# Gate and up projections as seven products of quarters

## The chip, the cores and the metric

The kernel runs on one core of a Trainium2 chip. The metric is the device time of one execution in microseconds (us). TensorE multiplies matrices into PSUM, VectorE, ScalarE and GpSimd (POOL in the profile) work on SBUF, the first two on PSUM as well, and SyncE (SP) issues the transfers from HBM. All five run on their own and wait for each other by semaphores.

## The reference

Two post-norm layers on 512 tokens of 1024 channels. Each layer has one projection with sparse attention and spatial gating, an output projection, a layer norm, then a feed-forward part of width 2816 with a gated term beside it, and a second layer norm:

```
x = layer_norm(ALPHA * x + mix, ln1_g, ln1_b)
gate, up = split(x @ w_ffn_in, 2)            # w_ffn_in: 1024 x 5632
ffn = (silu(gate) * up) @ w_ffn_out          # w_ffn_out: 2816 x 1024
ple = (p @ w_ple) * sigmoid(x @ w_ple_gate)
x = layer_norm(ALPHA * x + ffn + ple, ln2_g, ln2_b)
```

## The kernel before

All matmuls keep nearly float32 accuracy by splitting each operand into a high part (a rounded copy, type float32r) and a low part (the rest), and adding three products: high x high, high x low, low x high. `mm3` issues the three. The weights are split on the chip: `split` takes up to 1024 columns of a loaded tile, ScalarE casts the high part (`wh`), and VectorE or GpSimd subtracts it from the source to get the low part (`wl`). Activations are held transposed, channels on partitions and tokens along the columns, with both parts (`Rows`).

`ffn_in(j)` (11 times in a layer) computes 256 channels of the hidden layer: two loads of 1 MB (256 columns of gate and of up), four splits of 8 x 128 columns, for each of two channel tiles one bank of PSUM for gate and one for up, each the sum of 8 x 3 matmuls of 512 tokens. ScalarE takes Silu of gate, VectorE multiplies with up, and the product is split into the tiles `HT`. `ffn_out(f0, f1, last)` multiplies a group of hidden tiles with their rows of w_ffn_out, two halves of 512 output columns, each over four token blocks, and VectorE adds the banks into `X`. The groups are 8, 8 and 6 tiles, after passes 4, 8 and 10 of `ffn_in`. Ahead of the first pass stands the gate projection (`evac_g`, two halves of 512 columns), and ahead of that `evac_o1`, which normalizes a token block and transposes it into `X1T`.

Tiles come from pools: 15 big tiles (128 x 2048), 10 pages (128 x 512), two raw tiles for loaded weights, four pairs of `wh` and `wl`, four PSUM banks `acc` and three `ps`. Nothing is issued while the program is written down: `Order` records every operation, and `issue` then chooses the order of each engine by a list schedule. An operation has a key, the sum of the estimated TensorE time recorded before it; each engine takes, of those that could start within a short window of the earliest, the one with the lowest key. Tiles of one pool are given out in the order of the keys of their first operations. The order so found is fixed, and each engine runs through its own list, waiting where an operand is not there. All instructions are issued from one line of `issue`, so the profile shows L272 nearly everywhere, and rows are told apart by their tiles.

Of the kernel before, what the change touches and what calls it, by code (L numbers as in the profile page):

```python
# [326 lines left out]
def body(ctx: ExitStack, tc: tile.TileContext, x, p, positions, w_in, w_o, ln1_g, ln1_b,  # L327
# [20 lines left out]
    def ACC():  # L348
        return psum.tile([128, 512], F32, name="acc", tag="acc", bufs=4)
# [10 lines left out]
    def low(eng, dst, src, hi):  # L360
        eng.tensor_tensor(out=dst, in0=src, in1=f32(hi), op=OP.subtract)
# [113 lines left out]
    def wrows(w, r0, nkt, c0, c1):  # L475
        return w[r0:r0 + nkt * 128, c0:c1].rearrange("(k p) n -> p k n", p=128)

    def mform(xt, kts, load, ncols, order, evac, eng, c0=None, subs=None):


        ready = subs is not None
        subs = subs or []

        def fetch(i):
            if ready:
                return
            ks = kts[4 * i:4 * i + 4]
            rv = load(ks)
            for j in range(0, len(ks), 2):
                kk = ks[j:j + 2]  # L490
                subs.append((kk, split(rv[:, j:j + len(kk), :], [len(kk), ncols], eng)))

        nf = (len(kts) + 3) // 4

        def piece(b, acc, si):
            kk, (h, l) = subs[si]
            o = c0(b) if c0 else 0
            for j, k in enumerate(kk):
                mm3(acc[:, o:ncols], xt(k, b), (h[:, j, o:], l[:, j, o:]),
                    k == kts[0], k == kts[-1])  # L500

        if order == "k":
            accs = None
            done = 0
            for i in range(nf):
                fetch(i)
                if accs is None:
                    accs = [ACC() for _ in range(NB)]
                while done < len(subs):
                    for b in range(NB):  # L510
                        piece(b, accs[b], done)
                        if subs[done][0][-1] == kts[-1]:
                            evac(b, accs[b])
                        yield
                    done += 1
        else:
            for i in range(nf):
                fetch(i)
            for b in range(NB):
                acc = ACC()  # L520
                for si in range(len(subs)):
                    piece(b, acc, si)
                    if si == len(subs) - 1:
                        evac(b, acc)
                    yield

    def drive(main, *sides):
# [40 lines left out]
    def transpose_rows(R, b, src, halves=(0, 1)):  # L568
        for half in halves:
            ps = PS()  # L570
            for j in range(4):
                k = half * 4 + j
                PE.transpose(ps[:, j * 128:(j + 1) * 128], src[:, k * 128:(k + 1) * 128], ident)
            v = ps.rearrange("p (k t) -> p k t", k=4)
            s = slice(b * 128, (b + 1) * 128)
            A.copy(R.h[half][:, :, s], v)
            low(V, R.l[half][:, :, s], v, R.h[half][:, :, s])

    def rstd_of(src, n):

# [76 lines left out]
    for ly in range(DEPTH):  # L657
# [328 lines left out]
        X1T = Rows("x1t")  # L986

        def evac_o1(b, acc):
            xb = Xb(b)
            V.tensor_tensor(out=xb[:, 512:], in0=acc, in1=xb[:, 512:], op=OP.add)  # L990
            finish(layer_norm(xb, DM, lnp[:, 0], lnp[:, 1]))
            transpose_rows(X1T, b, xb)

        finish(mform(MT, [0, 1, 2, 3], load_o(1), 512, "b", evac_o1, G))

# [1 line left out]
        for n in range(2):  # L997
            cs = slice(n * 512, (n + 1) * 512)

            def evac_g(b, acc, n=n, cs=cs):  # L1000
                sg = PG(F32, "sg")
                A.activation(sg, acc, AF.Sigmoid)
                V.tensor_tensor(out=sg, in0=sg, in1=PLE[n][:, b], op=OP.mult)
                V.scalar_tensor_tensor(Xb(b)[:, cs], Xb(b)[:, cs], ALPHA, sg, op0=OP.mult, op1=OP.add)

            finish(mform(X1T, K8, mload(wg_l, n * 512, n * 512 + 512), 512,
                         "b" if n == 0 else "k", evac_g, G if n == 0 else V))


        HT = {}  # L1010

        def ffn_in(j):
            gr = raw(lambda t: [(t.rearrange("p (k n) -> p k n", k=8),
                                 wrows(wf_l, 0, 8, j * 256, j * 256 + 256))])
            ur = raw(lambda t: [(t.rearrange("p (k n) -> p k n", k=8),
                                 wrows(wf_l, 0, 8, DFF + j * 256, DFF + j * 256 + 256))])
            for e in range(2):
                f = 2 * j + e
                if f % 4 == 0:
                    HT[f // 4] = [T(FR, "HT").rearrange("p (k t) -> p k t", k=4) for _ in range(2)]  # L1020
                hh, hl = HT[f // 4]
                accs = []
                for r in (gr, ur):
                    w = split(r.rearrange("p (k n) -> p k n", k=8)[:, :, e * 128:e * 128 + 128],
                              [8, 128], V)
                    acc = ACC()
                    for k in range(8):
                        mm3(acc, (w[0][:, k], w[1][:, k]), X1T.all(k), k == 0, k == 7)
                    if not accs:
                        sg = PG(F32, "sg")  # L1030
                        A.activation(sg, acc, AF.Silu)
                    accs.append(acc)
                V.tensor_tensor(out=sg, in0=accs[1], in1=sg, op=OP.mult)
                A.copy(hh[:, f % 4], sg)
                low(V, hl[:, f % 4], sg, hh[:, f % 4])

        def hrow(f, b):
            bs = slice(b * 128, (b + 1) * 128)
            return HT[f // 4][0][:, f % 4, bs], HT[f // 4][1][:, f % 4, bs]

        def ffn_out(f0, f1, last):
            for n in range(2):
                cs = slice(n * 512, (n + 1) * 512)

                def evac_f(b, acc, n=n, cs=cs):
                    xb = Xb(b)
                    V.tensor_tensor(out=xb[:, cs], in0=acc, in1=xb[:, cs], op=OP.add)
                    if last and n == 1:
                        end = ly == DEPTH - 1
                        for c in layer_norm(xb, DM, lnp2[:, 0], lnp2[:, 1], 2 if end else 1):  # L1050
                            if end:
                                SY.dma_start(out[0, b * 128:(b + 1) * 128, c], xb[:, c])
                        if not end:
                            transpose_rows(XT, b, xb)

                finish(mform(hrow, list(range(f0, f1)), mload(wfo_l, n * 512, n * 512 + 512), 512,
                             "b" if last and n else "k", evac_f, G if last else V))

        for j in range(5):
            ffn_in(j)  # L1060
        ffn_out(0, 8, False)
        for j in range(5, 9):
            ffn_in(j)
        ffn_out(8, 16, False)
        for j in range(9, 11):
            ffn_in(j)
        lnp2 = T(F32, "lnp").rearrange("p (e c) -> p e c", e=2)
        row_bcast(lnp2[:, 0], ln2_g[ly], DM)
        row_bcast(lnp2[:, 1], ln2_b[ly], DM)
        if ly < DEPTH - 1:  # L1070
            subs_a = list(split_a([load_a(ly + 1, i) for i in range(2)], [V] * 4))
            XT = Rows("xt")
        ffn_out(16, 22, True)

    with tc.manual_schedule():
        order.issue()
# [22 lines left out]
```

## Time and profile before

| | |
|---|---|
| median of 3 runs | 1244.28 us (1243.76 to 1251.37) |
| profiled execution | 1247.03 us |
| its span, first to last instruction | 1245.3 us |
| mean granted clock of TensorE | 0.995 |
| TensorE, VectorE, ScalarE, GpSimd busy | 98%, 55%, 38%, 19% |
| read from HBM | 114.86 MB |

The span is that of the one profiled execution; its device time is 1.7 us longer. Busy shares are means over stages that differ, and a TensorE that is busy need not be at its full pace, since matmuls overlap in the records: one of 512 columns is shown with 389 ns while the next starts much sooner.

### The profile page before, as it was taken

Reading aid. Unit: us, or ns where it says so; the run is one execution under the profiler, and the core shown is the slowest. Engines: PE = TensorE matmul, PEld = TensorE weight load, DVE = VectorE, ACT = ScalarE, POOL = GpSimd, SP = SyncE. Lnnn points to the kernel's source line nnn. Section 1 sums busy time; section 2 is a strip of 40 time slices with the busy share of each in tenths; the row PEclk is TensorE's granted clock in tenths of the full one; section 3 lists DMA queues with packets and bytes.
Section 4 is the critical chain, followed back from the end, with each engine's and each line's share of the span. In section 5 each row is a group of like instructions: output and inputs, shape, how many; then the busy total and the mean of one; then the engine's idle time right before and its main releaser. Section 6 shows DMA issues by size and latency. Waiting matters only on the chain. (4 is left out here: it accounts for less than half of the span.)

```text
span 1245.3 us, 14733 instructions
## 1 busy us (share of the span) xinstructions
PE 1218.6 (98%) x5742; PEld 1008.8 (81%) x5742; DVE 683.7 (55%) x1334; ACT 473.5 (38%) x818; POOL 237.0 (19%) x186
## 2 busy tenths in 40 slices
PE   8989989999999999999999999999999999999997
PEld 8778768888888888888788888788888888888885
DVE  5699987853333333233487999785433333333317
ACT  5554686332222222213335558923322222222220
POOL 4135434400000000000552453460000000000042
PEclk9999999999999999999999999999999999999999
DMA  7123231242322323323411223313332324223231
GB/s 212 43 93 102 69 85 68 68 136 69 119 86 100 102 71 132 102 89 107 166 54 50 87 85 69 102 68 102 103 101 84 120 68 135 68 104 99 89 115 68
DMA packets 89621, 117.90 MB, mean 95 GB/s; under 512 B 5072, under 2 KB 59344, under 8 KB 89552
## 3 DMA queue, kind: packets, MB, share of 16 engines
q1 hardware_dynamic: 89552, 116.97, 29.5%
q8 instruction: 45, 0.74, 0.2%
q14 instruction: 24, 0.20, 0.1%
HBM read 114.86 MB, written 2.10 MB: 94 GB/s over the span
## 5 line engine op out<-in xcount | busy, mean ns | idle before, releaser
L272 POOL TENSOR_TENSOR wl<-raw,wh 128x512 fp32r<-128x512 f32 x132 | 181.6, 1403 | 888.9 <-ACT wh L272 877.0
L272 ACT CAST wh<-raw 128x1024 fp32r<-128x1024 f32 x194 | 202.8, 1050 | 382.3 <-PE acc L272 336.5
L272 DVE TENSOR_TENSOR wl<-raw,wh 128x1024 fp32r<-128x1024 f32 x128 | 156.8, 1225 | 307.5 <-ACT wh L272 307.3
L272 PE MATMUL acc<-x1th,wh 128*128 128x512 f32 x704 | 273.9, 389 | 0.0
L272 PE MATMUL acc<-x1tl,wh 128*128 128x512 f32 x704 | 273.9, 389 | 0.0
L272 PE MATMUL acc<-x1th,wl 128*128 128x512 f32 x704 | 273.9, 389 | 0.0
L272 PE MATMUL acc<-wh,HT 128*128 128x512 f32 x704 | 217.9, 389 | 0.5 <-ACT wh L272 0.5
L272 PEld LDWEIGHTS acc<-wh,HT 128*128 128x128 f32 x704 | 132.0, 188 | 28.1 <-ACT wh L272 0.9
L272 PEld LDWEIGHTS acc<-x1tl,wh 128*128 128x128 f32 x704 | 132.1, 188 | 27.6
L272 PEld LDWEIGHTS acc<-x1th,wl 128*128 128x128 f32 x704 | 132.1, 188 | 27.4
L272 PEld LDWEIGHTS acc<-x1th,wh 128*128 128x128 f32 x704 | 132.1, 188 | 27.3
L272 PE MATMUL acc<-wl,HT 128*128 128x512 f32 x352 | 137.3, 390 | 0.2 <-POOL wl L272 0.2
L272 ACT ACTIVATE sg<-acc 128x512 f32<-128x512 f32 x60 | 35.9, 598 | 189.7 <-PE acc L272 189.7
L272 DVE TENSOR_TENSOR sg<-acc,sg 128x512 f32<-128x512 f32 x44 | 30.4, 692 | 134.0 <-PE acc L272 134.0
L272 PE MATMUL acc<-wh,xth 128*128 128x512 f32 x192 | 76.3, 402 | 3.4 <-ACT rq L272 2.1
L272 PEld LDWEIGHTS acc<-wl,HT 128*128 128x128 f32 x352 | 66.1, 188 | 14.6 <-POOL wl L272 0.9
L272 PE MATMUL acc<-wl,xth 128*128 128x512 f32 x192 | 76.0, 398 | 0.0
L272 PE MATMUL acc<-wh,xtl 128*128 128x512 f32 x192 | 75.9, 396 | 0.0
L272 DVE TENSOR_TENSOR X<-acc,X 128x512 f32<-128x512 f32 x64 | 43.2, 685 | 43.5 <-PE acc L272 43.3
L272 DVE MATCH_REPLACE8 sc<-m,sc 128x384 f32<-128x384 f32 (+2 forms) x96 | 51.6, 541 | 0.0
L272 PE MATMUL acc<-wh,mth 128*128 128x512 f32 x128 | 51.3, 401 | 0.0
L272 PE MATMUL acc<-wh,mtl 128*128 128x512 f32 x128 | 51.3, 401 | 0.0
(197 smaller groups left out, 1705.4 us busy)
## 6 DMA issues: line engine op xcount, KB each, us to landing
raw<-in_w_ffn_in SPq DMA_DIRECT2D x44, 1024.0 KB, 5.1
raw<-in_w_ffn_out SPq DMA_DIRECT2D x20, 1024.0 KB, 5.0
raw<-in_w_in SPq DMA_DIRECT2D x12, 1024.0 KB, 5.3
raw<-in_w_ple_gate SPq DMA_DIRECT2D x8, 1024.0 KB, 5.0
raw<-in_w_o SPq DMA_DIRECT2D x4, 1024.0 KB, 5.3
raw<-in_w_o SPq DMA_DIRECT2D x8, 512.0 KB, 7.3
raw<-in_w_in SPq DMA_DIRECT2D x8, 324.0 KB, 4.7
X<-in_x SPq DMA_DIRECT2D x8, 256.0 KB, 5.1
```

Source lines behind the costliest of these rows:

```text
L272: o.ins = o.fn(*o.a, **o.k)
```

## The change

The input of the feed-forward part, X, is cut into four quarters: x11, x12 are the two channel halves of tokens 0 to 255, x21, x22 those of tokens 256 to 511. The weights of one pass are cut likewise: w11 and w21 are the channel halves of its 256 gate columns, w12 and w22 those of its 256 up columns. Instead of the eight products of quarters, seven are formed, from sums of quarters (the Winograd form of Strassen's scheme). The sums of X are made once in a layer (`combine`, beside the gate projection); those of the weights in every pass on VectorE, two into a new big tile `tt` and two in place over the raw tiles. A product is 2 channel tiles x 4 channel blocks x 3 matmuls of 256 tokens, its two channel tiles side by side in one bank. Bank `ba` takes four products in a row without being cleared; what it holds in between is copied or added out. `X1T` becomes an object `Quarters`, whose transposes also keep unsplit copies (`x1r`) until the sums are made. HT has one big tile for each pass. The down projection is done in groups of 6, 6, 4 and 6 tiles after passes 3, 6, 8 and 10 (counted from 0), all but the last with low parts on VectorE; the last group's loads and splits (`prefetch`, low parts on GpSimd) are recorded ahead of the next layer's first weights.

```diff
+    class Quarters:
+        def __init__(self):
+            self.q = [[self.tile("x1q") for _ in range(2)] for _ in range(2)]
+            self.raw = [T(F32, "x1r").rearrange("p (i k t) -> p i k t", i=4, k=4) for _ in range(2)]
...
+        def parts(self, t, i, src):
+            s = slice(i * 128, i * 128 + 128)
+            A.copy(t[:, 0, :, s], src)
+            low(V, t[:, 1, :, s], src, t[:, 0, :, s])
+        def rows(self, b, src):
...
+                self.parts(self.q[b // 2][half], i, v)
+                if b // 2 and half:
+                    V.tensor_tensor(out=self.raw[i][:, 3], in0=v, in1=self.raw[i][:, 2], op=OP.subtract)
+                else:
+                    A.copy(self.raw[i][:, 2 if b // 2 else half], v)
+        def combine(self):
+            self.sums = [self.tile("x1s") for _ in range(4)]
+            for i in range(2):
+                q11, q12, q21, p1 = (self.raw[i][:, j] for j in range(4))
+                self.parts(self.sums[0], i, p1)
+                yield
...
+                V.scalar_tensor_tensor(s2, p1, -1.0, q11, op0=OP.mult, op1=OP.subtract)
+                self.parts(self.sums[1], i, s2)
+                yield
+                V.tensor_tensor(out=s3, in0=q11, in1=q21, op=OP.subtract)
+                self.parts(self.sums[2], i, s3)
+                yield
+                V.scalar_tensor_tensor(s4, s2, -1.0, q12, op0=OP.mult, op1=OP.subtract)
+                self.parts(self.sums[3], i, s4)
+                yield
...
-            transpose_rows(X1T, b, xb)
+            X1T.rows(b, xb)
...
+            drive(mform(X1T, K8, mload(wg_l, n * 512, n * 512 + 512), 512,
+                        "b" if n == 0 else "k", evac_g, G if n == 0 else V), (comb, 0.25, 4))
+        finish(comb)
...
         def ffn_in(j):
...
+            w11, w21, w12, w22 = gr[:, 0:1024], gr[:, 1024:], ur[:, 0:1024], ur[:, 1024:]
+            tt = T(F32, "tt")
+            t1, t2 = tt[:, 0:1024], tt[:, 1024:]
+            t3, t4 = w12, w21
+            x11, x12, x22 = X1T.q[0][0], X1T.q[0][1], X1T.q[1][1]
+            xp, xs2, xs3, xs4 = X1T.sums
...
+            def product(bank, src, x, first):
+                h, l = split(src.rearrange("p (k n) -> p k n", k=4), [4, 256], V)
+                for e in range(2):
+                    dst = bank[:, e * 256:(e + 1) * 256]
+                    for k in range(4):
+                        cs = slice(e * 128, (e + 1) * 128)
+                        for n, (w_, x_) in enumerate(((h, 0), (h, 1), (l, 0))):
+                            PE.matmul(dst, w_[:, k, cs], x[:, x_, k], start=first and e + k + n == 0,
+                                      stop=k == 3 and n == 2, skip_group_check=True)
...
+            product(ba, w11, x11, True)
+            s1 = page_()
+            A.copy(s1, ba)
+            product(bb, w21, x12, True)
+            g1 = page_()
+            V.tensor_tensor(out=g1, in0=bb, in1=s1, op=OP.add)
+            A.activation(g1, g1, AF.Silu)
+            add(t1, w11, w12)
+            add(t2, t1, w22)
+            product(ba, t2, xs2, False)
+            s2 = page_()
+            A.copy(s2, ba)
+            bc = ACC()
+            product(bc, t1, xp, True)
+            s5 = page_()
+            A.copy(s5, bc)
+            add(t3, w22, w12)
+            product(ba, t3, xs3, False)
+            V.tensor_tensor(out=s5, in0=ba, in1=s5, op=OP.add)
+            product(bc, w22, xs4, False)
+            V.tensor_tensor(out=s2, in0=bc, in1=s2, op=OP.add)
+            add(t4, t2, w21)
+            product(ba, t4, x22, False)
+            g2 = page_()
+            A.activation(g2, ba, AF.Silu)
+            ht = HT[j] = T(FR, "HT").rearrange("p (e f t) -> p e f t", e=2, f=2)
+            for i, (g, u) in enumerate(((g1, s2), (g2, s5))):
+                V.scalar_tensor_tensor(u, u, -1.0, g, op0=OP.mult, op1=OP.mult)
+                v, ts = u.rearrange("p (f t) -> p f t", f=2), slice(i * 256, (i + 1) * 256)
+                A.copy(ht[:, 0, :, ts], v)
+                low(V, ht[:, 1, :, ts], v, ht[:, 0, :, ts])
...
+        for j in range(4):
             ffn_in(j)
-        ffn_out(0, 8, False)
-        for j in range(5, 9):
+        ffn_out(0, 6, False)
+        for j in range(4, 7):
             ffn_in(j)
-        ffn_out(8, 16, False)
+        ffn_out(6, 12, False)
+        for j in range(7, 9):
+            ffn_in(j)
+        ffn_out(12, 16, False)
         for j in range(9, 11):
             ffn_in(j)
...
+        subs_o = [prefetch(load_fo(n), list(range(16, 22)), 512, G) for n in range(2)]
...
-        ffn_out(16, 22, True)
+        ffn_out(16, 22, True, subs_o)
```

## Rows read from the trace of the kernel before

**Rows 1.** The page, busy us, share of the span and instructions of each engine.
```profile
PE 1218.6 (98%) x5742; PEld 1008.8 (81%) x5742; DVE 683.7 (55%) x1334; ACT 473.5 (38%) x818; POOL 237.0 (19%) x186
```

**Rows 2.** Windows: busy time by engine, over gate and up, then a down projection.
```profile
core 0: us, PE busy (x) PEld busy (x) DVE busy (x) ACT busy (x) POOL busy (x), PEclk, DMA share, GB/s
271.00:380.00 109.00, 109.00 (x483) 90.25 (x482) 39.17 (x43) 32.56 (x42) 0.00 (x0) 1.00 0.32 105
380.00:431.00 51.00, 51.00 (x227) 42.23 (x226) 17.48 (x19) 11.25 (x12) 0.00 (x0) 1.00 0.31 103
```

**Rows 3.** Timeline (start, duration, engine) of TensorE: first and last of 92 matmuls.
```profile
469.22 0.39 PE L272 MATMUL acc<-x1tl,wh 128*128 128x512 f32 x1
...
489.85 0.39 PE L272 MATMUL acc<-x1th,wl 128*128 128x512 f32 x1
```

**Rows 4.** Timeline of TensorE, two runs of matmuls of 256 columns.
```profile
119.17 2.67 PE L272 MATMUL ps<-vn,wsT 128*128 128x256 f32 x21
...
810.02 2.07 PE L272 MATMUL po<-PT,VV 128*128 128x256 f32 x16
```

**Rows 5.** Timeline of the weight loads: those of the second run, and one.
```profile
809.56 0.19 PEld L272 LDWEIGHTS acc<-wh,mtl 128*128 128x128 f32 x1
809.79 2.09 PEld L272 LDWEIGHTS po<-PT,VV 128*128 128x128 f32 x16
```

**Rows 6.** Timeline of VectorE around `ffn_in`, and two operations on one block.
```profile
442.20 1.23 DVE L272 TENSOR_TENSOR wl<-raw,wh 128x1024 fp32r<-128x1024 f32 x1 [4.32 <-ACT wh L272]
...
446.99 1.22 DVE L272 TENSOR_TENSOR wl<-raw,wh 128x1024 fp32r<-128x1024 f32 x1 [0.22 <-ACT wh L272]
448.13 0.68 DVE L272 TENSOR_TENSOR HT<-sg,HT 128x512 fp32r<-128x512 f32 x1
...
222.94 1.27 DVE L272 TENSOR_TENSOR x1tl<-ps,x1th 128x512 fp32r<-128x512 f32 x2
```

**Rows 7.** Timeline of ScalarE in the same stretch.
```profile
445.90 1.05 ACT L272 CAST wh<-raw 128x1024 fp32r<-128x1024 f32 x1 [3.73 <-PE acc L272]
446.86 0.62 ACT L272 CAST HT<-sg 128x512 fp32r<-128x512 f32 x1
```

**Rows 8.** Timeline of SP's queue, a load issued in the same stretch.
```profile
443.46 0.37 SPq L272 DMA_DIRECT2D raw<-in_w_ffn_in  x1
```

**Rows 9.** The page, DMA issues: count, KB each, median us from issue to landing.
```profile
raw<-in_w_ffn_in SPq DMA_DIRECT2D x44, 1024.0 KB, 5.1
```

**Rows 10.** Groups of instructions with busy us and mean ns: transposes into X1T.
```profile
L272 ACT CAST x1th<-ps 128x512 fp32r<-128x512 f32 x16 | 8.6, 590 | 28.8 <-PE ps L272 28.7
...
L272 DVE TENSOR_TENSOR x1tl<-ps,x1th 128x512 fp32r<-128x512 f32 x16 | 10.2, 680 | 0.0
```

**Rows 11.** Windows over the gate projection of the first layer.
```profile
230.00:241.60 11.60, 11.35 (x58) 9.23 (x57) 11.50 (x17) 4.87 (x8) 5.80 (x4) 1.00 0.26 90
241.60:245.40 3.80, 3.80 (x18) 3.14 (x18) 0.04 (x1) 0.60 (x1) 0.00 (x0) 1.00 0.00 0
245.40:271.00 25.60, 25.60 (x115) 21.19 (x114) 13.14 (x15) 9.43 (x11) 0.00 (x0) 1.00 0.30 91
```

**Rows 12.** Timeline of TensorE in that stretch, its one wait.
```profile
231.08 0.49 PE L272 MATMUL acc<-wh,x1tl 128*128 128x512 f32 x1 [0.25 <-DVE x1tl L272]
```

**Rows 13.** Timeline of SP's queue before the first layer's last down projection.
```profile
574.01 6.70 SPq L272 DMA_DIRECT2D raw<-in_w_in  x8
...
592.61 0.38 SPq L272 DMA_DIRECT2D raw<-in_w_ffn_out  x1
```

**Rows 14.** Timeline of ScalarE there, the casts of that load.
```profile
597.73 2.94 ACT L272 CAST wh<-raw 128x1024 fp32r<-128x1024 f32 x3 [3.99 <-DMA raw<-in_w_ffn_out]
```

**Rows 15.** Timeline of TensorE there, its longest wait.
```profile
598.83 1.20 PE L272 MATMUL acc<-wh,HT 128*128 128x512 f32 x4 [0.47 <-ACT wh L272]
```

**Rows 16.** Timeline of TensorE after its longest wait in the first projections.
```profile
71.77 0.79 PE L272 MATMUL acc<-wh,xth 128*128 128x512 f32 x1 [2.08 <-ACT rq L272]
```

**Rows 17.** Windows over that stretch; the 0.50 is the granted clock.
```profile
71.70:74.90 3.20, 3.13 (x7) 2.48 (x8) 3.20 (x12) 0.02 (x1) 1.51 (x2) 0.50 0.22 19
```

More of the change, by code (lines that the diff above doesn't have):

```diff
@@ L525, in mform, with prefetch @@
                     yield
+    def prefetch(load, kts, ncols, eng):
+        subs = []
+        for i in range(0, len(kts), 4):
+            ks = kts[i:i + 4]
+            rv = load(ks)
+            for j in range(0, len(ks), 2):
+                kk = ks[j:j + 2]
+                subs.append((kk, split(rv[:, j:j + len(kk), :], [len(kk), ncols], eng)))
+        return subs
     def drive(main, *sides):
@@ L577, in transpose_rows, with tile, __call__ @@
             low(V, R.l[half][:, :, s], v, R.h[half][:, :, s])
+    class Quarters:
+        def __init__(self):
+            self.q = [[self.tile("x1q") for _ in range(2)] for _ in range(2)]
+            self.raw = [T(F32, "x1r").rearrange("p (i k t) -> p i k t", i=4, k=4) for _ in range(2)]
+            self.sums = None
+        def tile(self, name):
+            return T(FR, name).rearrange("p (e k t) -> p e k t", e=2, k=4)
+        def __call__(self, k, b):
+            t, s = self.q[b // 2][k // 4], slice(b % 2 * 128, b % 2 * 128 + 128)
+            return t[:, 0, k % 4, s], t[:, 1, k % 4, s]
+        def parts(self, t, i, src):
[3 more added lines that the diff above has]
+        def rows(self, b, src):
+            i = b % 2
+            for half in range(2):
+                ps = PS()
+                for j in range(4):
+                    k = half * 4 + j
+                    PE.transpose(ps[:, j * 128:(j + 1) * 128], src[:, k * 128:(k + 1) * 128], ident)
+                v = ps.rearrange("p (k t) -> p k t", k=4)
+                self.parts(self.q[b // 2][half], i, v)
[9 more added lines that the diff above has]
+                yield
+                s2, s3, s4 = (PG(F32, "s").rearrange("p (k t) -> p k t", k=4) for _ in range(3))
+                V.scalar_tensor_tensor(s2, p1, -1.0, q11, op0=OP.mult, op1=OP.subtract)
[7 more added lines that the diff above has]
+                yield
     def rstd_of(src, n):
@@ L985, in body @@
         finish(mform(MT, [0, 1, 2, 3], load_o(0), 512, "b", evac_o0, G))
-        X1T = Rows("x1t")
+        X1T = Quarters()
         def evac_o1(b, acc):
@@ L1004, in evac_g @@
                 V.scalar_tensor_tensor(Xb(b)[:, cs], Xb(b)[:, cs], ALPHA, sg, op0=OP.mult, op1=OP.add)
-            finish(mform(X1T, K8, mload(wg_l, n * 512, n * 512 + 512), 512,
-                         "b" if n == 0 else "k", evac_g, G if n == 0 else V))
+            if n == 0:
+                comb = X1T.combine()
+            drive(mform(X1T, K8, mload(wg_l, n * 512, n * 512 + 512), 512,
+                        "b" if n == 0 else "k", evac_g, G if n == 0 else V), (comb, 0.25, 4))
+        finish(comb)
@@ L1010, in body @@
         HT = {}
         def ffn_in(j):
-            gr = raw(lambda t: [(t.rearrange("p (k n) -> p k n", k=8),
-                                 wrows(wf_l, 0, 8, j * 256, j * 256 + 256))])
+            c0 = j * 256
+            gr = raw(lambda t: [(t.rearrange("p (k n) -> p k n", k=8), wrows(wf_l, 0, 8, c0, c0 + 256))])
             ur = raw(lambda t: [(t.rearrange("p (k n) -> p k n", k=8),
[L1016 to L1035, printed above, removed]
@@ new lines, in ffn_in, with add @@
+                                 wrows(wf_l, 0, 8, DFF + c0, DFF + c0 + 256))])
+            w11, w21, w12, w22 = gr[:, 0:1024], gr[:, 1024:], ur[:, 0:1024], ur[:, 1024:]
[4 more added lines that the diff above has]
+            xp, xs2, xs3, xs4 = X1T.sums
+            def add(out, a, b):
+                V.tensor_tensor(out=out, in0=a, in1=b, op=OP.add)
+            def product(bank, src, x, first):
[7 more added lines that the diff above has]
+                                      stop=k == 3 and n == 2, skip_group_check=True)
@@ new lines, in page_ @@
+            def page_():
+                return PG(F32, "fg")
+            ba, bb, bc = ACC(), ACC(), None
+            product(ba, w11, x11, True)
[9 more added lines that the diff above has]
+            s2 = page_()
@@ L1037, in hrow @@
+            ht = HT[j] = T(FR, "HT").rearrange("p (e f t) -> p e f t", e=2, f=2)
[4 more added lines that the diff above has]
+                low(V, ht[:, 1, :, ts], v, ht[:, 0, :, ts])
         def hrow(f, b):
             bs = slice(b * 128, (b + 1) * 128)
-            return HT[f // 4][0][:, f % 4, bs], HT[f // 4][1][:, f % 4, bs]
@@ L1041, in ffn_out, with load_fo @@
-        def ffn_out(f0, f1, last):
+            return HT[f // 2][:, 0, f % 2, bs], HT[f // 2][:, 1, f % 2, bs]
+        def load_fo(n):
+            return mload(wfo_l, n * 512, n * 512 + 512)
+        def ffn_out(f0, f1, last, subs=(None, None)):
             for n in range(2):
@@ L1054, in evac_f @@
                             transpose_rows(XT, b, xb)
-                finish(mform(hrow, list(range(f0, f1)), mload(wfo_l, n * 512, n * 512 + 512), 512,
-                             "b" if last and n else "k", evac_f, G if last else V))
-        for j in range(5):
+                finish(mform(hrow, list(range(f0, f1)), load_fo(n), 512,
+                             "b" if last and n else "k", evac_f, V, subs=subs[n]))
+        for j in range(4):
             ffn_in(j)
-        ffn_out(0, 8, False)
-        for j in range(5, 9):
+        ffn_out(0, 6, False)
+        for j in range(4, 7):
             ffn_in(j)
-        ffn_out(8, 16, False)
+        ffn_out(6, 12, False)
+        for j in range(7, 9):
+            ffn_in(j)
+        ffn_out(12, 16, False)
         for j in range(9, 11):
```

## The prediction

> **What bounds the kernel now.** The page's busy shares come first: TensorE 98%, VectorE 55%, ScalarE 38% [rows 1]. Taken by stage, the window over the gate and up projections shows TensorE busy all of its 109 us, VectorE 39 us, ScalarE 33 us, at a granted clock of 1.00, and the window over a down projection shows the same picture, 51.0 us against 17.5 and 11.3 [rows 2]. Busy TensorE is not yet proof of a full pace, so the order of its matmuls is read: 92 matmuls of 512 columns in a row start from 469.22 to 489.85, one each 0.2267 us, with no step at a change of weights, bank or tile [rows 3]. So in this stage the time is the number of matmuls by 0.2267 us, and each other engine waits. What counts is whether the new matmuls keep a steady pace, and whether VectorE, which receives nearly all that the change adds, stays hidden.
>
> **TensorE.** One pass of `ffn_in` has 2 channel tiles x 2 projections x 8 x 3 = 96 matmuls of 512 columns: 96 x 0.2267 = 21.76 us. After, it has 7 products x 2 x 4 x 3 = 168 of 256 columns. The trace has that shape with new weights each time: 21 in 2.67 us and 16 in 2.07 us [rows 4]. The last one's own length, about 0.28 us, comes off, so they start each (2.67 - 0.28)/20 = 0.1195 us. A pass is 168 x 0.1195 = 20.08 us, 1.687 less. With 11 passes in each of 2 layers, 22 x 1.687: **-37.1 us**. (A half-width matmul costs 0.527 of a full one, so of the eighth that the algebra saves 7.7% is left.)
>
> Each new matmul has its own load of weights, and a load lasts longer than the matmul's share: 16 loads take 2.09 us, (2.09 - 0.19)/15 = 0.127 us from one to the next, though one lasts 0.19 [rows 5]. So they lie over each other and over the matmuls before. The Trainium skill speaks against that: "TensorE: Matmul & The Clock Gate", Part 3, has loads overlap matmuls in flight only where the row group is another one, and here every load fills all rows. By that rule the sum would be that of the third rival below; these rows do not agree with it.
>
> **VectorE in a pass.** Before: 4 low parts of 1024 elements, and 4 operations of 512. After: 7 low parts, 4 sums of weights of the same shape, and 7 of 512 (three bank additions, two multiplications, two low parts of HT). Alone, one of 1024 takes 1.225 us and one of 512 about 0.69. Packed they start closer: the operation after a low part starts 1.14 us after it, and two of 512 end 1.27 us after the first starts, so 0.60 each [rows 6]. Packed, a pass is 11 x 1.14 + 7 x 0.60 = 16.7 us; alone, 13.5 + 4.8 = 18.3. Both are below 20.08, so load by itself does not bind. ScalarE has 7 casts at 0.96 (start to start) and 7 of 0.6, 10.9 us [rows 7]: hidden.
>
> **The order inside a pass.** I walk it with E_n for the end of product n, 24 x 0.1195 = 2.87 us apart. Four buffers hold split weights, so the cast for product n+4 starts at E_n, its low part 1.09 us later, done at E_n + 2.3 [rows 6, 7]. Of the two raw buffers, the up half is last read by split 6, done at E2 + 2.3, the gate half by split 7, at E3 + 2.3. A transfer is issued 0.03 us after such a low part ends, and the cast starts 5.1 us after the issue [rows 6, 8, 9, 13, 14]. So the next pass's first cast is at E4 + 1.7, its low part at E5, and its second half is there at E5 + 1.7. Between E3 + 2.3 and E5 VectorE has nothing, 3.4 us, and 16.7 + 3.4 = 20.1 is the whole pass: no reserve. One thing more pushes: big tiles are handed out in the order of their first use, so the next tt (t1, t2) waits for the first cast into this pass's HT, about E6 + 1.75. Behind a late t1 stand t2 and the split of t2, and product 3 waits for that. Placing each operation from there, t2, t3, the split of t2 and the others in line, I find the second pass of a group still ready for every product, by 0.4 us at the tightest; the third has t2 split about 1 us late, the fourth somewhat more. The first pass of a group is free: a down projection or the gate goes ahead, where a buffer lasts 24 x 0.2267 = 5.4 us, so that three splits and all sums are done. Groups have 4, 3, 2 and 2 passes, so 3 passes in each layer are late: 6 x 1.2 = **+7 us**. Ends: 0, if the casts and sums interleave better, and for all 14 passes that are not first, the second rival's price.
>
> **Gate projection.** Per layer come 6 casts and 2 subtractions in the transposes, then `combine`: 8 casts, 14 VectorE operations of 512. At 0.59 and 0.68 [rows 10] that is 8.3 us of ScalarE and 10.9 of VectorE. In this stage VectorE is busy 11.5 of the first 11.6 us, then free for 3.8 and half free after, and TensorE already waits 0.25 for a low part [rows 11, 12]. `combine` is keyed behind the norms, so it should fill the free part. What lies on the path are the 2 subtractions among the last norms, 1.4 us: I take 1.5 a layer, **+3 us**. Ends: nothing, and all 10.9 a layer; a gain is excluded, since nothing is taken out there.
>
> **Edits at nothing.** A fourth call of `ffn_out` adds 8 additions into X a layer, 5.5 us of VectorE, under matmuls that leave it two thirds idle [rows 2]; without that cover it would cost those 5.5. The last down projection's splits are put ahead of the next layer's: its 4 transfers go before 8 of w_in on SP's queue. Before, the order was w_in at 574.0, w_ffn_out at 592.6, its cast at 597.7, and TensorE waited 0.47 us for it [rows 13 to 15]. That may come back; w_in then arrives later, hidden by 6 x 24 matmuls (32.6 us) of down projection; uncovered, its 18.6 us of delay would be the price. POOL keeps the same low parts.
>
> **Sum.** The profiled execution took 1247.03 us (span 1245.3 and 1.7 around it), 2.75 above the median. 1247.03 - 37.1 + 7 + 3 = 1219.9, and 1217 on the median's footing. A stall of 2 us can cost more than itself: after 2.08 us without a matmul the granted clock is 0.50, which is 1.2 GHz, for 3.2 us, in which 7 matmuls start in place of 14 [rows 16, 17]. The stalls that I expect are shorter.
>
> **Rivals.**
> First, VectorE keeps up altogether: the planner places the sums in idle stretches, the tt tile comes early, the norms lose nothing. Then 1244.3 - 37.1 = 1207. For it: packed load is 83% of a pass. Against: the 3.4 us hole. 20%.
> Second, and to the other side: **VectorE's reload hole sets the pass.** Place: between the low part of split 6 and the first low part of the next pass, 5.1 + 1.09 us, of which only split 7 fills 1.2. If operations also run at their lone length because each waits for a cast or a bank, a pass is 18.3 + 5.0 = 23.3 us, 1.55 more than now. With 14 such passes, 8 free ones at -1.68, and the gate: 14 x 1.55 - 13.4 + 3 = +11, so 1255. It decides from a pass of 22.5 us on, where 14 x 0.74 equals what the free passes leave. For it: every low part in the present stage starts after a wait for its cast, 4.32 and 0.22 us [rows 6]. Against: a saturated engine has other work to put there. Milder forms lie between 1232 and 1255. 25%, a little over half of it within 1% of before.
> Third, weight loads bind in a long run: 168 x 0.19 = 31.9 us a pass, 10.2 more than now, about 1244 + 223 = 1467. It needs [rows 4, 5] not to carry over from 21 matmuls to 24 and more. 3%.
>
> **Numbers.** My forecast, 1211 to 1230, has 52%. Faster by over 1% (what a measurement of this kernel can tell) means below 1231.8: forecast and first rival, 0.72. Within 1%: 0.14, the milder half of the second rival. Slower: 0.11 of the second and the third, 0.14. The range goes from 1206, the first rival, to 1244, which leaves out the worse half of the second rival, the third, and 3% below.
>
> **What would show it.** Matmuls of 256 columns each 0.12 us, 7 x 24 of them in 20.1 us in the first pass of each group: right; 0.19 apart: third rival. Waits of TensorE for wh or wl in third and fourth passes, about 1 us at t2's split: the forecast; in every second pass, of 3 us, at the first split after a transfer: second rival; none: first. VectorE should be near 80 to 90% busy in the passes with one hole of about 3 us around the transfer. In the gate, TensorE's waits for x1q should sum to 1 to 2 us a layer. What would make it wrong above all is an order written by the planner that puts sums ahead of a low part that is due, which no row of before can show.

## The result and the profile after

The changed kernel takes 1215.76 us (median of 4, 1214.99 to 1217.81) against 1246.09 before in the same measurements: a ratio of 0.9753, 95% interval 0.9717 to 0.9789. That is 2.5% faster, beside 1217 predicted. The profiled execution's span falls from 1245.3 to 1214.2 us, by 31.1.

The page of the kernel after, busy time by engine, against [rows 1]:

```profile
PE 1184.2 (98%) x7326; PEld 1055.1 (87%) x7326; DVE 931.2 (77%) x1602; ACT 593.5 (49%) x978; POOL 238.4 (20%) x186
```

TensorE is as busy as before for a shorter time. VectorE has 248 us more of work and ScalarE 120, and the kernel is faster all the same. The three passes of the second group of the first layer, as windows of the kernel after (us, then each engine's busy time and count, the granted clock, transfers), answer to [rows 2]:

```profile
387.35:407.51 20.16, 20.16 (x170) 20.15 (x169) 11.89 (x13) 9.00 (x11) 0.00 (x0) 1.00 0.32 105
407.51:427.67 20.16, 20.16 (x171) 20.16 (x170) 16.69 (x18) 11.03 (x14) 0.00 (x0) 1.00 0.33 105
427.67:447.83 20.16, 20.16 (x171) 20.16 (x170) 16.91 (x19) 11.93 (x15) 0.00 (x0) 1.00 0.28 84
```

Each pass is 20.16 us, where one took 21.76. VectorE (the third pair) has less to do in the first pass, whose sums were made ahead, and 16.7 of 20.16 us in the second. The timeline of TensorE shows the pace; the first row is the first matmul of that second group, the last the first matmul of its second pass, 168 later, so they start each 20.16/168 = 0.1200 us:

```profile
387.35 0.40 PE L272 MATMUL acc<-x1q,wh 128*128 128x256 f32 x2
...
407.51 0.40 PE L272 MATMUL acc<-x1q,wh 128*128 128x256 f32 x2
```

Where the 31.1 us come from, by stages cut at the first matmul of the gate, the first of `ffn_in` and the last of the down projection:

| stage (both layers) | before | after | difference |
|---|---|---|---|
| up to the gate, and the tail | 430.45 | 430.13 | -0.3 |
| gate projection | 46.91 + 46.93 | 47.37 + 47.39 | +0.9 |
| passes and down projections | 362.18 + 358.81 | 347.21 + 342.10 | -31.7 |

22 passes at 20.16 give 443.5 us; the 22 passes after sum to 446.7, so 3.2 us are gaps. All the gaps stand at the third product of a pass, the one with t2, and all in the first group of a layer, in its second, third and fourth pass. The largest one, in the timeline of TensorE of the kernel after, below the first matmul of its pass (in brackets the wait and what ended it):

```profile
332.63 0.40 PE L272 MATMUL acc<-x1q,wh 128*128 128x256 f32 x2
...
338.27 0.28 PE L272 MATMUL acc<-x1q,wl 128*128 128x256 f32 x1
339.07 0.50 PE L272 MATMUL acc<-x1s,wh 128*128 128x256 f32 x2 [0.51 <-ACT fg L272]
340.44 0.39 PE L272 MATMUL acc<-x1s,wl 128*128 128x256 f32 x1 [0.88 <-DVE wl L272]
```

The second wait is for the low part of t2, which comes 0.88 us after TensorE could use it. The first, 0.51 us, is for ScalarE's copy of bank `ba`, which stands behind the cast of t2 in ScalarE's order, so it comes from a late t2 as well. What goes ahead, on ScalarE and then on VectorE:

```profile
329.23 2.00 ACT L272 CAST wh<-raw 128x1024 fp32r<-128x1024 f32 x2 [4.14 <-DMA raw<-in_w_ffn_in]
...
336.96 1.05 ACT L272 CAST wh<-tt 128x1024 fp32r<-128x1024 f32 x1 [1.81 <-DVE tt L272]
...
338.44 0.58 ACT L272 COPY fg<-acc 128x512 f32<-128x512 f32 x1
```

```profile
330.31 2.36 DVE L272 TENSOR_TENSOR wl<-raw,wh 128x1024 fp32r<-128x1024 f32 x2 [2.48 <-ACT wh L272]
...
333.92 1.22 DVE L272 TENSOR_TENSOR tt<-raw 128x1024 f32<-128x1024 f32 x1
...
339.17 2.35 DVE L272 TENSOR_TENSOR wl<-tt,wh 128x1024 fp32r<-128x1024 f32 x2
```

ScalarE waits 4.14 us for the transfer and VectorE for ScalarE; t1 (333.92) starts 1.29 us into its pass. The late passes have their first transfer issued 10.3 us ahead of them; those that follow another pass and have no gap, 11.0 to 12.0 us. VectorE's timeline over one pass without a gap, where t1 starts 1.35 us ahead of the pass (407.51), the kernel after:

```profile
405.55 0.69 DVE L272 SCALAR_TENSOR_TENSOR fg<-fg 128x512 f32<-128x512 f32 x1
406.16 1.22 DVE L272 TENSOR_TENSOR tt<-raw 128x1024 f32<-128x1024 f32 x1
407.30 0.68 DVE L272 TENSOR_TENSOR HT<-fg,HT 128x512 fp32r<-128x512 f32 x1
407.90 1.22 DVE L272 TENSOR_TENSOR tt<-tt,raw 128x1024 f32<-128x1024 f32 x1
409.04 0.68 DVE L272 SCALAR_TENSOR_TENSOR fg<-fg 128x512 f32<-128x512 f32 x1
409.64 1.22 DVE L272 TENSOR_TENSOR raw<-raw 128x1024 f32<-128x1024 f32 x1
410.81 0.69 DVE L272 TENSOR_TENSOR HT<-fg,HT 128x512 fp32r<-128x512 f32 x1
411.41 2.35 DVE L272 TENSOR_TENSOR wl<-tt,wh 128x1024 fp32r<-128x1024 f32 x2
...
416.55 1.22 DVE L272 TENSOR_TENSOR raw<-tt,raw 128x1024 f32<-128x1024 f32 x1
418.94 1.23 DVE L272 TENSOR_TENSOR wl<-raw,wh 128x1024 fp32r<-128x1024 f32 x1 [1.17 <-ACT wh L272]
422.18 0.69 DVE L272 TENSOR_TENSOR fg<-acc,fg 128x512 f32<-128x512 f32 x1 [2.01 <-PE acc L272]
423.13 2.36 DVE L272 TENSOR_TENSOR wl<-raw,wh 128x1024 fp32r<-128x1024 f32 x2 [0.26 <-ACT wh L272]
```

Read it from t1 (406.16): t1, a low part of HT, t2, t3 and the rest of HT stand packed ahead of the low parts of t2 and t1 (411.41), 1.14 and 0.60 us apart. Then comes a loose stretch, waits of 1.17, 2.01 and 0.26 us around the next transfer. The last row is the next pass's first pair of splits.

### The profile page after: what moved, and what is told of

It is laid out like the page before. It is cut to its first block, busy times and chain, and to the rows that moved or that the text cites. A ratio compares the mean times of both kernels' runs of the same rounds, so it can differ in the third digit from the quotient of the medians.

```text
span 1214.2 us, 18437 instructions
## 1 busy us (share of the span) xinstructions
PE 1184.2 (98%) x7326; PEld 1055.1 (87%) x7326; DVE 931.2 (77%) x1602; ACT 593.5 (49%) x978; POOL 238.4 (20%) x186
## 5 line engine op out<-in xcount | busy, mean ns | idle before, releaser
L272 PE MATMUL acc<-x1s,wh 128*128 128x256 f32 x1408 | 254.7, 283 | 0.5 <-ACT fg L272 0.5
L272 PEld LDWEIGHTS acc<-x1s,wh 128*128 128x128 f32 x1408 | 219.6, 192 | 0.7 <-ACT fg L272 0.7
L272 PE MATMUL acc<-x1s,wl 128*128 128x256 f32 x704 | 199.8, 284 | 1.0 <-DVE wl L272 0.9
L272 PE MATMUL acc<-x1q,wh 128*128 128x256 f32 x1056 | 191.3, 283 | 0.0
L272 PEld LDWEIGHTS acc<-x1q,wh 128*128 128x128 f32 x1056 | 165.2, 192 | 0.6
L272 PEld LDWEIGHTS acc<-wh,HT 128*128 128x128 f32 x704 | 132.0, 188 | 27.1
L272 PE MATMUL acc<-x1q,wl 128*128 128x256 f32 x528 | 149.4, 283 | 0.0
L272 PEld LDWEIGHTS acc<-x1s,wl 128*128 128x128 f32 x704 | 135.1, 192 | 2.2 <-DVE wl L272 2.2
L272 PEld LDWEIGHTS acc<-x1q,wl 128*128 128x128 f32 x528 | 101.3, 192 | 0.0
L272 ACT CAST wh<-tt 128x1024 fp32r<-128x1024 f32 x44 | 46.2, 1051 | 80.3 <-PE acc L272 61.6
L272 PE MATMUL acc<-wh,x1q 128*128 128x512 f32 x256 | 80.4, 392 | 0.5 <-DVE x1q L272 0.5
```

The source lines that it names most:

```text
L272: o.ins = o.fn(*o.a, **o.k)
```

## The experiments

First the gaps of all runs, from the timelines of TensorE: the 22 passes summed, what is over 443.5, and where nearly all of it stands.

| kernel | passes, us | over 443.5 | at product | longest pass |
|---|---|---|---|---|
| after | 446.7 | 3.2 | 3 | 22.1 |
| without sums of weights | 445.7 | 2.1 | 7 | 21.1 |
| eleven passes in a row | 452.5 | 9.0 | 3 | 22.7 |
| t1 and t2 twice | 490.0 | 46.5 | 3 | 26.8 |
| four additions ahead of t2's split | 492.7 | 49.2 | 3 | 28.3 |
| four additions in the hole | 447.0 | 3.5 | 3 | 21.9 |
| three raw buffers | 443.5 | 0.0 | none | 20.2 |
| t1 and t2 twice, three raw buffers | 469.5 | 26.0 | 3 | 22.0 |
| HT used ahead of tt | 505.8 | 62.2 | 3 | 28.1 |
| HT used right after t1 | 455.9 | 12.4 | 3 and 7 | 24.8 |
| groups of 8, 8 and 6 | 449.1 | 5.6 | 3 | 23.8 |
| without combine | 447.0 | 3.5 | 3 and 7 | 21.7 |

**Matmuls of half the width, alone.** In the kernel before:

```diff
-                    for k in range(8):
-                        mm3(acc, (w[0][:, k], w[1][:, k]), X1T.all(k), k == 0, k == 7)
+                    for t2 in range(2):
+                        ts = slice(t2 * 256, (t2 + 1) * 256)
+                        for k in range(8):
+                            xh, xl = X1T.all(k)
+                            mm3(acc[:, ts], (w[0][:, k], w[1][:, k]), (xh[:, ts], xl[:, ts]), k == 0, k == 7)
```

> The kernel before with each matmul of ffn_in cut into two of 256 columns, the same products in all: 192 matmuls a pass. Theory (256 columns start each 0.120 us at any length of run): 192 x 0.120 = 23.04 us a pass against 21.76, 22 x 1.28 = +28 us, 1274. Rival (weight loads bind in a long run): 192 x 0.19 = 36.5 us a pass, +320 us.

1275.17 us, a ratio to before of 1.0228 (1.0197 to 1.026), and the two stages with the passes are 15.2 and 14.1 us longer. The 28 us are there, the matmuls start each 0.120 us, and the loads of weights do not bind: this is the price that the algebra pays first.

**Without the sums of weights.**

```diff
-            tt = T(F32, "tt")
-            t1, t2 = tt[:, 0:1024], tt[:, 1024:]
-            t3, t4 = w12, w21
+            t1, t2, t3, t4 = w12, w22, w12, w21
...
-            add(t1, w11, w12)
-            add(t2, t1, w22)
...
-            add(t3, w22, w12)
...
-            add(t4, t2, w21)
```

> The changed kernel without its four sums of weights in each pass; the products take plain quarters instead, so what is computed is not the reference. VectorE loses 4 x 1.14 us a pass, the loads and the raw buffers stay as they are. Theory (the few stalls left in the passes come from the chain load, t1, t2, split of t2): TensorE's matmuls of ffn_in then start each 0.120 us without a gap over 0.1 us in all 22 passes, and the time falls by the 3.3 us that the gaps sum to, 1216 to 1212.5. Rival (VectorE still costs time elsewhere in the passes): a fall of over 8 us. Rival (the gaps come from late transfers alone): the gaps stay.

1215.21 us, ratio 0.975 (0.9733 to 0.9767), the same as with the sums. The gaps at product 3 are gone, as the theory said, but 2.1 us of others stand at product 7, so the fall of 3.3 did not come. The 88 sums, 100 us of VectorE, cost about 1 us of the passes on balance.

**Eleven passes in a row.**

```diff
-        for j in range(4):
-            ffn_in(j)
-        ffn_out(0, 6, False)
...
+        for j in range(11):
+            ffn_in(j)
```

> The changed kernel with all 11 passes of a layer in a row: the down projections of the first 16 hidden tiles are left out, so what is computed is not the reference, and the time means nothing; the length of a pass does. Theory (hole and chain nearly fill a pass): passes 5 to 11 settle at 20.4 to 21.0 us where TensorE's own pace is 20.16, with the gap at the product with t2. Rival 1 (the reload hole sets the pass once no down projection goes ahead): 22.5 to 23.3 us. Rival 2 (VectorE keeps up altogether): 20.16 in every pass.

In its one execution, passes 5 to 11 take 20.4 us on the mean in the first layer and 20.6 in the second, each gap at t2. The middle reading holds: without down projections between them, passes settle 1 to 2% over TensorE's own pace, far from 22.5.

**More VectorE work in three places.** Twice t1 and t2; then four additions of 512, recorded behind t2; then the same four behind the copy of bank bc:

```diff
+            add(t1, w11, w12)
...
+            add(t2, t1, w22)
```

```diff
+            for i in range(4):
+                k = i % 2 * 2
+                V.tensor_tensor(out=page_().rearrange("p (k t) -> p k t", k=2), in0=f32(x11[:, 0, k:k + 2]),
+                                in1=f32(x12[:, 0, k:k + 2]), op=OP.add)
```

> The changed kernel with t1 and t2 each computed twice, in the place where they stand: 2.28 us more of VectorE a pass, in the chain from the transfer to the split of t2. Theory (that chain is what binds behind the reload hole): the second and later passes of a group lose up to 2.3 us each, less the slack of the first: +10 to +25 us, 1226 to 1241. Rival (VectorE has free time enough): +0 to +4 us.

> The changed kernel with four additions of 512 elements more in each pass, which nothing reads, 2.4 us of VectorE off every chain. Theory (the reload hole of about 3 us is free time that other work can fill): +0 to +5 us, much less than with the same load in the chain. Rival (VectorE's load as such is at its edge, wherever it stands): the same loss as with the load in the chain.

> The changed kernel with four additions of 512 elements more in each pass, which nothing reads, recorded behind the copy of bank bc, so that they are due where VectorE waits for the next transfer: 2.4 us a pass, and not ahead of the split of t2 as in the run off every chain. Theory (the reload hole is free time, and what costs is only what stands between the transfer and t2's split): +0 to +6 us to the changed kernel, 1216 to 1222. Rival (VectorE's load as such is at its edge): +40 us and more, as in the two runs with the same load in other places.

Twice t1 and t2: 1259.97 us, ratio to before 1.0099 (1.0073 to 1.0126). That is 44 us over the changed kernel and more than either theory gave. The four additions behind t2: 1263.78, 1.014 (1.0121 to 1.0159); the rival is what was measured, but the run was not what its text said. The timeline of VectorE in that kernel shows where the planner put them:

```profile
295.07 1.22 DVE L272 TENSOR_TENSOR tt<-tt,raw 128x1024 f32<-128x1024 f32 x1
...
297.34 1.22 DVE L272 TENSOR_TENSOR raw<-tt,raw 128x1024 f32<-128x1024 f32 x1
298.48 0.69 DVE L272 TENSOR_TENSOR fg<-acc,fg 128x512 f32<-128x512 f32 x1
299.07 2.49 DVE L272 TENSOR_TENSOR fg<-x1q 128x512 f32<-128x512 f32 x4
301.48 2.36 DVE L272 TENSOR_TENSOR wl<-tt,wh 128x1024 fp32r<-128x1024 f32 x2
```

They are recorded before the low part of t2 and stand right ahead of it: no operand ties them to the chain, their place in an engine's fixed order does. The rest of the order has changed with them: t4 (297.34) and a bank addition, which the kernel after has behind the split of t2, stand ahead of it too. In 6 of the 22 passes the additions stand ahead of that split, and these lose 5.9 to 8.1 us each, 44.7 in all; in the other 16 they stand behind it, and these lose 4.5 in all. The 6 suffer from the pass before as well: there the additions stand ahead of the splits that set the raw tiles free, and t1 of the 6 starts 2.0 to 3.8 us into its pass.

Hence the third run: 1217.73 us, ratio 0.9765 (0.9742 to 0.9789), passes of 447.0. There VectorE carries the four additions in its loose stretch:

```profile
326.06 1.23 DVE L272 TENSOR_TENSOR wl<-raw,wh 128x1024 fp32r<-128x1024 f32 x1 [1.17 <-ACT wh L272]
327.21 2.49 DVE L272 TENSOR_TENSOR fg<-x1q 128x512 f32<-128x512 f32 x4
329.62 0.68 DVE L272 TENSOR_TENSOR fg<-acc,fg 128x512 f32<-128x512 f32 x1
331.55 2.36 DVE L272 TENSOR_TENSOR wl<-raw,wh 128x1024 fp32r<-128x1024 f32 x2 [1.25 <-ACT wh L272]
```

The same 2.4 us a pass cost 0.3 us over all passes in one place, and 46 in the other, together with the order that came of it and the clock (below). So VectorE's load is not at its edge; the queue ahead of t2's split is, and ahead of the splits that set the raw tiles free.

In the kernel with t1 and t2 twice, single passes lost 6.6 us for 2.28. Part of that is the order again, on VectorE in the second pass of the first layer:

```profile
298.16 1.22 DVE L272 TENSOR_TENSOR tt<-tt,raw 128x1024 f32<-128x1024 f32 x1
299.29 0.68 DVE L272 TENSOR_TENSOR fg<-acc,fg 128x512 f32<-128x512 f32 x1
299.89 1.22 DVE L272 TENSOR_TENSOR raw<-tt,raw 128x1024 f32<-128x1024 f32 x1
301.02 2.35 DVE L272 TENSOR_TENSOR wl<-tt,wh 128x1024 fp32r<-128x1024 f32 x2
```

A bank addition and t4 stand between the second t2 and the split. Another part is the clock. Timeline of TensorE and windows of the same pass (the third number from the end of a window is the granted clock):

```profile
300.56 0.80 PE L272 MATMUL acc<-x1s,wh 128*128 128x256 f32 x2 [2.92 <-ACT wh L272]
302.03 0.80 PE L272 MATMUL acc<-x1s,wh 128*128 128x256 f32 x2 [0.67 <-ACT wh L272]
302.63 0.41 PE L272 MATMUL acc<-x1s,wl 128*128 128x256 f32 x1
302.84 0.63 PE L272 MATMUL acc<-x1s,wh 128*128 128x256 f32 x2
```

```profile
293.00:300.50 7.50, 4.64 (x39) 4.43 (x37) 7.50 (x10) 2.20 (x5) 0.00 (x0) 0.98 0.00 0
300.50:304.00 3.50, 2.77 (x11) 2.47 (x12) 3.50 (x4) 3.38 (x5) 0.00 (x0) 0.50 0.00 0
304.00:308.00 4.00, 4.00 (x24) 4.00 (x24) 1.65 (x2) 0.61 (x2) 0.00 (x0) 0.62 0.26 76
```

After a gap of 2.92 us the clock is 0.50, 1.2 GHz, as in [rows 16, 17], and matmuls start 0.21 us apart (302.63 to 302.84); the 0.62 is the mean of a stretch that ends at the full 2.4 GHz. In the 7.5 us that follow, TensorE does 35 matmuls where 7.5/0.1200 = 62 would fit; the wait of 0.67 us accounts for 6 of those missing. By the starts of its matmuls, about 4.0 of the 6.6 us are the two waits and 2.6 the slower matmuls. Over the whole kernel, the matmuls in a row at 0.21 us cost 7.7 of the 46.5 us.

**Three raw buffers.**

```diff
-    page = ctx.enter_context(tc.tile_pool(name="page", bufs=10))
-    rawp = ctx.enter_context(tc.tile_pool(name="raw", bufs=2))
+    page = ctx.enter_context(tc.tile_pool(name="page", bufs=6))
+    rawp = ctx.enter_context(tc.tile_pool(name="raw", bufs=3))
```

> The changed kernel with three raw buffers in place of two, and 6 pages in place of 10 to make room. The gate half of the next pass can then be loaded while both halves of this one are in use, so the reload hole goes. Theory (the hole is what brings the chain late): no gaps at t2 in any pass, -3 us, 1213, if 6 pages do not hold anything up. Rival (the VectorE chain is late by itself): gaps as before. Price of the fewer pages: 0 to +10 us outside the passes, seen in the other stages.

1208.16 us (1206.85 to 1209.5), ratio to before 0.9695 (0.9669 to 0.972): faster than the kernel before, and 0.6% under the changed kernel, whose runs lie at 1214.99 to 1217.81. All 22 passes take 20.16 us, so the late transfer is what brings t2 late in the changed kernel, as its lines above show too. Only 3.2 us of the gain is from there: the stage up to the first gate is 7.2 us shorter (224.22 to 217.03) and the one between the layers 2.9 longer, which has nothing to do with the seven products and was not taken apart.

**Both together**: the doubled t1 and t2 with three raw buffers.

> Three raw buffers and 6 pages, with t1 and t2 each computed twice: VectorE has the same 2.28 us more a pass in the same chain as in the run that lost 44 us. Theory (what costs is the chain behind a late transfer, and a third raw buffer brings the transfer a pass ahead): passes sum to 443.5 to 452 us, the time is 1208 to 1217. Rival (VectorE's load is at its edge): passes of 21 to 22 us, 1240 to 1255.

1237.76 us, ratio 0.9924 (0.9906 to 0.9943). The theory fails. The rival is right in the passes, not in the time, which lies under its 1240: every pass that is not first in its group takes 22.0 us, 14 x 1.86 in all, with no transfer to wait for. But what binds is not load, as the run above showed. In the two kernels with three raw buffers t1 starts at one same point. VectorE's t1 and ScalarE's first cast into HT, three raw buffers:

```profile
303.38 1.22 DVE L272 TENSOR_TENSOR tt<-raw 128x1024 f32<-128x1024 f32 x1
```

```profile
303.50 0.62 ACT L272 CAST HT<-fg 128x512 fp32r<-128x512 f32 x1 [3.35 <-DVE fg L272]
```

In the kernel with both it is 307.89 and 308.00, in the changed kernel 406.16 and 406.28. Both come right behind the same multiplication on VectorE, and t1 starts 1.34 or 1.35 us ahead of its pass each time. That fits the order of the big tiles; the next runs try it. From there the chain has a reserve until product 3: in the pass from 407.51 the low part of t2 ends at 412.63 and TensorE's first matmul with it starts at 413.51, where in the pass with the largest gap it starts 0.05 us after such an end. That leaves 0.8 us. In the kernel with both the low part ends 2.8 us later, 2.28 for the doubled sums and the rest for a bank addition that the planner put ahead of the split.

**The order of the big tiles.** The tile HT is taken at the head of the pass, and one element of it written early, first behind product 1 (which I got wrong: it puts HT ahead of the same pass's tt), then behind t1:

```diff
             A.copy(s1, ba)
+            A.copy(ht[:, 0, 0, 0:1], s1[:, 0:1])
```

```diff
             add(t1, w11, w12)
+            A.copy(ht[:, 0, 0, 0:1], t1[:, 0:1])
```

> The changed kernel with one element of HT written by ScalarE right after the first product of a pass, so that HT is first used before the next pass's tt, and tt is not held back by the order in which big tiles are given out. Theory (that order makes t1 1 to 1.5 us late): t1 starts right after the two low parts of the pass's first transfer, the gaps at t2 vanish or halve, -1.5 to -3 us, 1213. Rival (t1 waits for VectorE's queue, not for its tile): no difference over 0.5 us in the passes.

> The changed kernel with one element of HT written by ScalarE right after t1 of the same pass, which puts the first use of HT between this pass's tt and the next pass's, and early. Theory (t1 is held back by the order in which big tiles are given out, since tt follows the HT of the pass before): t1 can start when its transfer has landed, about 1.2 us earlier in the trace after; the gaps at the product with t2, 3.3 us in all, fall to under 1.5. Rival (VectorE's own queue holds t1): gaps of 3 us or more. A third: the early HT fills the big pool, and passes get longer.

The first holds tt back: t1 starts 0.8 to 5.1 us into its own pass. 1274.78 us, ratio 1.0224 (1.0191 to 1.0258), every pass longer, the opposite of what I expected and a sign of how hard a late t1 is punished. The second frees it: in that kernel a t1 starts at 311.31, and the HT cast of the pass before only at 313.18; in the second groups t1 starts up to 2.95 us ahead of its pass. So the order of the big tiles does hold t1. But the time is 1226.55 us, ratio 0.9842 (0.982 to 0.9864): the gaps grow to 12.4 us, now also at product 7. The planner uses the freedom to make other choices, in the first groups with t3 and t4 behind the splits of t2 and t1. There the two transfers of the third pass are issued 1.28 us apart, the second takes 8.0 us to land, and t1 comes later than in the changed kernel. Whether another order with an early t1 would gain stays open.

**Groups as before, 8, 8 and 6 tiles.**

```diff
-        for j in range(4):
+        for j in range(5):
             ffn_in(j)
-        ffn_out(0, 6, False)
+        ffn_out(0, 8, False)
...
```

> The changed kernel with the down projections in the groups of before, 8, 8 and 6 tiles after 5, 4 and 2 passes. Theory (a group pays from its third pass on, and at five passes the big pool holds 5 HT beside 9 tiles, which leaves one for tt): the fifth pass is late by 2 to 6 us, the fourth by 0.5 to 2, +4 to +14 us in all. Rival (a pass costs the same wherever it stands): +0 to +1 us.

1219.18 us, ratio 0.9773 (0.9739 to 0.9807): not to be told from the changed kernel. The passes are 2.4 us longer, 1.8 of it in one fourth pass (23.8); the fifth passes take 20.2 and 20.4. The theory was right in sign at most.

**Without copies and combine.**

```diff
-                if b // 2 and half:
-                    V.tensor_tensor(out=self.raw[i][:, 3], in0=v, in1=self.raw[i][:, 2], op=OP.subtract)
-                else:
-                    A.copy(self.raw[i][:, 2 if b // 2 else half], v)
...
-            xp, xs2, xs3, xs4 = X1T.sums
+            xp, xs2, xs3, xs4 = X1T.q[1][0], x11, x12, x22
...
-                        "b" if n == 0 else "k", evac_g, G if n == 0 else V), (comb, 0.25, 4))
-        finish(comb)
```

> The changed kernel without the unsplit copies and without combine: the products take quarters of X instead of their sums, so what is computed is not the reference. It takes 8.3 us of ScalarE and 10.9 us of VectorE out of each gate stage. The trace after shows that stage 0.46 us longer than before in each layer: by that the stage shortens by 0.5 us, from 47.4 to 46.9. By the prediction's term it would be 1.5 a layer. Rival (the load also makes the first group's passes late): the gaps in the first group vanish too, 2.6 and 0.9 us.

In its one execution the gate stages take 46.89 and 46.95 us, those of before to within 0.02. So copies and combine cost 0.46 us a layer there, not 1.5. Of the gaps at product 3, all in the first groups, 2.0 us are left of 3.2, so the rival is neither borne out nor excluded; 1.5 us at product 7 of one pass are new.

## Why the prediction was right, step by step

- **The sum.** A fall of 27.1 us was forecast (1247.03 to 1219.9); the spans fell by 31.1 and the medians by 30.3. That 1217 lies 1.2 us from 1215.76 is luck in part: the terms were off by 1.8 us one way and by 3.8 and 2.1 the other, and the median of the kernel before, from which 1217 was counted, is 1.8 us higher in these measurements.
- **TensorE.** -37.1 predicted; the pace is 0.1200 and not 0.1195 us, so 22 x (20.16 - 21.763) = -35.3. The run with half the width alone confirms the price of the width, and neither it nor the kernel after shows loads of weights that bind: the third rival is out. The Trainium skill ("TensorE: Matmul & The Clock Gate", Part 3), which has loads overlap matmuls in flight only where the row group is another one, is not borne out here: these loads fill all rows and last 0.19 us each, and matmuls start each 0.1200 us all the same.
- **VectorE in a pass.** 16.7 us packed predicted, 16.69 measured in a second pass. "Both are below 20.08, so load by itself does not bind": shown by the additions in the hole.
- **The order inside a pass.** The product that is late, t2's, was named rightly. What was wrong is the sum, +7 against 3.2, and where it stands. "3 passes in each layer are late" came out as a number by luck. It counted the third pass of the second group, which has no gap in either layer; and the second passes, held to be ready "by 0.4 us at the tightest", have 0.8 us of reserve outside the first groups and lose 0.26 and 0.22 us in them. Of the 3.2 us, 1.9 are one pass whose transfer landed late. The transfers of weights of the kernel after that were issued at 301.89 and 322.36 us, for the third pass and for the fourth of the first layer, KB and median us from issue to landing:

```profile
raw<-in_w_ffn_in SPq DMA_DIRECT2D x1, 1024.0 KB, 5.2
```

```profile
raw<-in_w_ffn_in SPq DMA_DIRECT2D x1, 1024.0 KB, 6.8
```

  The second of them came 1.6 us later than the first, and the fourth pass is the one of 22.1. In four other kernels that transfer took 6.6 to 7.5 us too. That the next one is issued 3.5 us behind it is not the reason, since this holds for the one at 301.89 as well; why it is slower is open.
- "3.4 us, and 16.7 + 3.4 = 20.1 is the whole pass: no reserve" was wrong as an argument. A hole is not lost if later work can be put there, and 2.4 us of additions went into it for 0.3. The reserve is in the queue from t1 to t2's split, and there it is 0.8 us.
- "One thing more pushes: big tiles are handed out in the order of their first use": true of t1's start. That it makes passes late in the changed kernel is not shown, since freeing it made them longer.
- **Gate.** +3 predicted, +0.9 measured: the two subtractions among the norms do not lie on the path with their full length. TensorE waits 0.5 us for x1q in both layers together, where 1 to 2 us a layer were named as the sign.
- **The moved splits.** The wait of 0.47 us is gone, as allowed, and a new one of 1.44 us stands at 612.19, where transposes for the next layer wait for VectorE's X. Undoing that move alone was not tried.
- **First and second rival.** Passes without any gap, the first rival's, came only with three raw buffers. The second's 23.3 us does not come even in eleven passes in a row. It was right that the reload matters, since a third raw buffer removes the gaps; but TensorE waits at t2's split, and not at the first split after a transfer as it said.

## What to carry to other kernels

Saved products must be priced at the new shape's measured pace: an eighth fewer multiplications were 7.4% of a pass here, because a matmul of half the width takes 0.1200 us and not half of 0.2267. An engine at 83% can hide 2.4 us more in each pass or cost 46 us by them, and the busy share doesn't tell which: look for the packed stretch ahead of the operation that the bound engine needs next, and put what is not urgent into the loose one. Here, where the gap follows a transfer, a third buffer did more than rearranging the sums.

## What was not expected of the hardware

The clock's answer to a gap makes small delays grow. A gap of 2.92 us was followed by 3.5 us at 0.50 and by 4 us at 0.62 on the mean, and of the 6.6 us that this pass lost about 2.6 are slower matmuls. Shorter waits were enough in the kernel with groups of 8, 8 and 6: behind waits of 0.79 and 0.88 us, ended at 341.97 and 343.36, the clock stood at 0.52 on the mean over 2.8 us. In the changed kernel it stayed at 1.00 behind waits of 0.51 and 0.88 us (339.07 and 340.44). In the kernel with both edits, where a late pass has waits of 0.28 to 0.45 us, it stayed at 1.00 as well, and the doubled sums cost 1.86 us in each of these passes.
